# Moving the weight sums of a seven-product matrix scheme from VectorE to GpSimd, with more blocks under the scheme

## The chip, the cores and the metric

One core of one Trainium2 chip. Times are device microseconds for one launch of the whole program; the kernel before has a median of 2390.53 us over three runs.

## The reference

A two-layer encoder over one sequence of 256 tokens with 2048 features, all in float32. Each layer is a norm, a token mixer, a residual add, then a norm, a gated feed-forward part and a residual add. The change lies in the feed-forward part alone:

```python
def conv_glu(hn, w_up, conv_w, conv_b, w_down):
    u = hn @ w_up                       # 256 x 2048 times 2048 x 11008
    a, v = jnp.split(u, 2, axis=-1)
    ...                                 # c: depthwise convolution of width 3 over tokens
    return (jax.nn.gelu(c, approximate=False) * v) @ w_down     # 256 x 5504 times 5504 x 2048
```

## The kernel before

**Numbers in two halves.** TensorE multiplies in a reduced float32 form. Every operand is split into a high part, a cast by ACT (`wh`, `th`), and a low part, the difference made by VectorE (`wl`, `tl`). A product of two operands is then three matmuls: high by high, high by low, low by high (`product`, L237).

**Weights as a stream.** All weights pass through one stream of chunks. A raw piece of 128 x 2048 is loaded into one of three buffers `raw` by SP's queue, and split 1024 columns at a time into four buffers `wh` (L137, ACT) and `wl` (L138, VectorE). `stream` asks for pieces three ahead (`LOOK`). A scheduler orders the instructions of each engine when the program is built.

**Up and down chunks.** The feed-forward part of a layer works in two parts: 22 blocks of 128 hidden features, then 21. For each block there is an up chunk (32 pairs of matmuls at L328 and L332, then some ten small operations of VectorE and ACT, `done_up`, that give the block of activations `GT`). Behind the up chunks of a part come down chunks. Those of kind "st" compute a pair of 512-column outputs at once, from two blocks of hidden features (a unit) and both halves of the tokens: the first pair of columns in both parts (`w_d0`), the second pair in part 0 alone (`w_d1`). The rest of part 1 goes in ordinary chunks. So a layer has three such down chunks of 11 units; in part 1 the last unit is half as large.

**Units and couples.** A unit is a product of 2 x 2 blocks, A (activations) by B (weights). A regular unit takes eight products. A couple, one of the units listed in `SEVEN`, takes seven, by Strassen's scheme in Winograd's form: it needs four sums of weight blocks (T1 to T4, `weight_sums`) and four of activation blocks (S1 to S4, `token_sums`), each split in halves too. Four products' sums are kept in the PSUM tiles `psm_` over the whole chunk and added to the residual `hm` by `mid` behind the last couple (L546 to L554, the last two by GpSimd); the four `psa_` are added by `done` (L559).

**Where the weight sums are made.** For the six units in `STORED` of every down chunk, VectorE makes the sums during the up chunks. `prepare` is a side job with due times: `side` has a clock of its own, advanced as matmuls are issued by 10.4 per up chunk in ticks of 0.65, and a job that yields a number goes on that much later. It loads the couple's weights into `pth` (1 MB), makes three differences (L179, L182, L184: T1 to T4 in `ptl`), and stores 1 MB into a scratch tensor `tscr` in DRAM. In the down chunk `split_squares` loads them back (`T<-tscr`), and ACT and VectorE split them (`th`, L209; `tl`, L210). The block B12 itself is then not needed, so that a stored unit's raw piece has 1536 columns. Unit 9 of part 0's first chunk is not stored; its sums are made in the down chunk. The loads and stores share SP's queue with the raw loads, in order: an instruction that waits holds those behind it. The down chunk's first pieces are issued once `prepare` is through; what is left of it then is issued at once (`side.until`).

Of the kernel before, what the change touches and what calls it, by code (L numbers as in the profile page):

```python
# [48 lines left out]
SEVEN = (1, 2, 4, 5, 7, 8, 9), (1, 2, 4, 5, 7, 8), (1, 2, 4, 5, 7, 8)  # L49
STORED = (1, 2, 4, 5, 7, 8)  # L50
# [10 lines left out]
def trunk_kernel(ctx, tc, xT, x_d, fg_d, pp_d, cst_d, w_gate, w_first, w_aq, w_ak, w_av, w_ao, w_aout, w_ao2,  # L61
# [114 lines left out]
    def weight_sums(a, b, T, T_):  # L176

        B22, B21, B12 = a[:, 512:1024], b[:, 0:512], b[:, 512:1024]
        dve.tensor_tensor(T.rearrange("p (a b) -> p a b", a=2), B12.unsqueeze(1).broadcast_to([P, 2, 512]),  # L179
                          a.rearrange("p (a b) -> p a b", a=2), ALU.subtract)  # L180
        yield 2.5
        dve.tensor_tensor(T_[:, 0:512], B22, T[:, 0:512], ALU.subtract)  # L182
        yield 2.5
        dve.tensor_tensor(T_[:, 512:1024], B21, T_[:, 0:512], ALU.subtract)  # L184

    def split_squares(ch, parts):
# [4 lines left out]
        def raw(u):  # L191
            if u not in raws and u < units:
                raws[u] = load_raw(ch.src, 2048 * u, min(2048 * (u + 1), 1024 * ch.nk) - (512 if u in ch.stored else 0))
                if u in ch.stored:
                    kept[u] = [temporary(ch.pool, "T") for _ in range(2)]
                    for t, src in zip(kept[u], ch.stored[u]):
                        nc.sync.dma_start(t, src)
            return raws.get(u)

        def combine(u):  # L200
            r = raw(u)
            T, T_ = kept[u] if u in kept else (temporary(ch.pool, "T") for _ in range(2))
            if u not in kept:
                for _ in weight_sums(r[:, 0:1024], r[:, 1024:2048], T, T_):
                    pass
            sums[u] = []
            for i, t in enumerate((T, T_)):
                th, tl = (ch.pool.tile([P, 1024], F32R, tag=n, name=n) for n in (f"th{i}", f"tl{i}"))
                act.copy(th, t)  # L209
                dve.tensor_tensor(tl, t, th.bitcast(F32), ALU.subtract)  # L210
                sums[u].append((th, tl))

        for u in range(units):
            r = raw(u)
            if u + 1 in ch.seven and not ch.late:
                combine(u + 1)
            wh, wl = parts(r[:, 0:1024], 1024)
            yield wh, wl, 1
            if u + 1 in ch.seven and ch.late:
                combine(u + 1)  # L220
            if 2 * u + 1 < ch.nk:
                m = 512 if u in ch.seven else 1024
                wh, wl = parts(r[:, 1024:1024 + m], m)
                yield wh, wl, sums.pop(u, None)

    def squares_by_seven(ch, fetch, ready):
# [20 lines left out]
        for u in range(units):  # L247
# [3 lines left out]
            if 2 * u + 1 == ch.nk:  # L251
# [4 lines left out]
                break  # L256
            fetch()
            q = ready.pop(0)
            x0, x1 = ch.x(2 * u), ch.x(2 * u + 1)
            A11, A21, A12, A22 = half(x0, 0), half(x0, 1), half(x1, 0), half(x1, 1)  # L260
            B11, B22, B21 = block(p[:2], 0), block(p[:2], 1), block(q[:2], 0)
            if u in ch.seven:
                sx, t = ch.sums(u), q[2]
                S1, S3, S2, S4 = ((sx[:, i * P:(i + 1) * P], sx[:, 512 + i * P:512 + (i + 1) * P]) for i in range(4))
                T1, T3, T2, T4 = (block(t[i // 2], i % 2) for i in range(4))
                for i, (ps, x, w) in enumerate(((P1, A11, B11), (C12, S4, B22), (C11, A12, B21), (P5, S1, T1),
                                                (P7, S3, T3), (P6, S2, T2), (C21, A22, T4))):
                    product(ps, x, w, u == last and ps in psm_)
                    side.tick(0.65)
# [257 lines left out]
    def token_sums(mp, i, a, b, S):  # L527

        sx = mp.tile([P, 1024], F32R, tag=f"sx{i}", name="sx")
# [3 lines left out]
        act.copy(sx[:, 0:512], S)  # L533
        dve.tensor_tensor(sx[:, 512:1024], S, sx[:, 0:512].bitcast(F32), ALU.subtract)
        return sx
# [37 lines left out]
    def prepare(mp, todo, period, finished):  # L573

        yield 24.0
        for src, dst in todo:
            r, T = ([mp.tile([P, 1024], F32, tag=f"{n}{i}", name=f"p{n}") for i in range(2)] for n in ("th", "tl"))
            for i in range(2):
                late(r[i], src[:, i * 1024:(i + 1) * 1024])
            yield 9.0  # L580
            yield from weight_sums(*r, *T)
            for i in range(2):
                nc.sync.dma_start(dst[i], T[i])
            yield max(1.0, period - 14.0)
# [512 lines left out]
    def ffn(layer, norm, nxt):  # L1097
        stack = ExitStack()
        box = dict(n=3 * len(STORED) * layer)
# [10 lines left out]
        def done_up(f, i, GT, SX, seven):  # L1110
            def go(ps):
# [15 lines left out]
                if i % 2 and i // 2 in seven:  # L1127
                    SX[i // 2] = token_sums(mp, seven.index(i // 2), box["c"], c, avc[:, 0:2 * T])
# [3 lines left out]
        for part, (f0, nf) in enumerate(((0, FA), (FA, FB))):  # L1132
            GT, SX, todo, finished = [], {}, [], []

            def prep(todo=todo, finished=finished, nf=nf):
                if not pairs[0].pool:
                    begin()
                side.push(prepare(box["mp"], todo, (nf * 10.4 - 24.0) / len(todo) - 1.5, finished))

            for i in range(nf):  # L1140
                chunks.append(Chunk("fm", w_up[layer, f0 + i], KT, norm.x, done_up(f0 + i, i, GT, SX, SEVEN[2 * part]),
                                    prep if i == 0 else None,
                                    swap=(2,) if part and i == 0 else (3,) if f0 + i == 1 else (), paced=True))
            def two(src, c0, norm, seven, GT=GT, SX=SX, nf=nf, todo=todo, finished=finished):
                ch = pair(src, nf, c0, lambda k: GT[k], lambda u: SX[u], norm, seven)
                for u in STORED:
# [7 lines left out]
            chunks.append(two(w_d0[layer][:, f0 * 1024:(f0 + nf) * 1024], 0, nxt if part else None, SEVEN[2 * part]))  # L1154
# [4 lines left out]
            else:  # L1159
                chunks.append(two(w_d1[layer], 2, None, SEVEN[1]))  # L1160
# [103 lines left out]
def build(nc, ins, out_shape=(2, P, D), **kw):  # L1264
# [4 lines left out]
    tscr = nc.dram_tensor("tscr", (6 * len(STORED), 2, P, 1024), F32, kind="Internal").ap()  # L1269
# [18 lines left out]
```

## Time and profile before

| | |
|---|---|
| median of three runs | 2390.53 us (2390.34 to 2392.72) |
| span of the profiled execution, first to last instruction | 2388.5 us |
| TensorE busy | 2372.4 us, 99% |
| VectorE busy | 1944.1 us, 81% |
| ACT busy | 1298.8 us, 54% |
| GpSimd busy | 189.7 us, 8% |
| bytes read and written in DRAM | 512.69 MB, 39.91 MB |
| granted TensorE clock | 0.999 |

The runs give times of launches; the profiled execution is known by its span, and the median lies 2.0 us above that. In the profile's rows PE is TensorE, PEld its weight loads, DVE VectorE, POOL GpSimd, SP the queue that issues most DMAs, and L137 is line 137 of the kernel. A row of a group gives busy time, the mean time of one in ns, and behind the second bar the idle time of the engine before such instructions with what ended it.

### The profile page before, as it was taken

The page shows a single profiled execution, that of the slowest core. Times are in us where ns is not written, and L with a number is a line of the kernel's source. Part 1 is how long each engine was busy: PE and PEld are TensorE (multiplying, and loading weights), DVE is VectorE, ACT ScalarE, POOL GpSimd, SP SyncE. Part 2 cuts the span into 40 slices and gives each one's busy share as a digit, 9 for nine tenths or more (in the row PEclk, how much of TensorE's full clock was granted, in tenths as well). Part 3 has the DMA queues.
Part 4 walks back from the last instruction along what each step waited for, and adds up shares of the span by engine and source line. Part 5 has one row for each costly group of instructions (what it writes and reads, how often), then busy time and mean ns, then how long its engine had stood idle before and what let it go on. Part 6 is the DMA issues. An engine that isn't in the chain of part 4 may idle for free.

```text
span 2388.5 us, 37988 instructions
## 1 busy us (share of the span) xinstructions
PE 2372.4 (99%) x14614; PEld 2030.4 (85%) x14614; DVE 1944.1 (81%) x3221; ACT 1298.8 (54%) x2013; POOL 189.7 (8%) x240
## 2 busy tenths in 40 slices
PE   9999999999999999999999999999999999999998
PEld 7888888888888888888888888888888888888887
DVE  7766687988887888777888888888889888788874
ACT  7655455454564554555555555555555565454563
POOL 0100000000000000001222222220000000000000
PEclk9999999999999999999999999999999999999999
DMA  8654556988787777755554554545798888677774
GB/s 300 201 180 165 183 178 211 333 294 317 269 293 254 251 239 262 273 194 182 173 171 168 175 177 160 177 166 188 258 325 298 298 281 296 231 249 263 249 266 148
DMA packets 98789, 555.07 MB, mean 232 GB/s; under 512 B 11168, under 2 KB 11680, under 8 KB 50736
## 3 DMA queue, kind: packets, MB, share of 16 engines
q1 hardware_dynamic: 96912, 548.64, 65.6%
q0 software_dynamic: 1120, 3.21, 0.7%
q8 instruction: 114, 1.87, 0.3%
q10 hardware_dynamic: 576, 0.79, 0.1%
q14 instruction: 67, 0.55, 0.1%
HBM read 512.69 MB, written 39.91 MB: 231 GB/s over the span
## 4 chain that ended last, share of the span: by engine, by line
PE 98%; DVE 1%; issue 1%; DMA 0%; ACT 0%; SPq 0%; POOLq 0%; POOL 0%
PE mm L328 37%; PE mm L344 23%; PE mm L332 18%; PE pc L237 12%; PE mm L237 5%; PE pn L776 1%; PE py L1034 1%; PE pd L984 1%; PE pz L405 0%; PE pa L984 0%; DMA raw<-in_w_first 0%; PE S L762 0%; DVE tl L210 0%; PE pz L1055 0%; PE pa L1009 0%
## 5 line engine op out<-in xcount | busy, mean ns | idle before, releaser
L328 PE MATMUL mm<-xt,wh 128*128 128x512 f32 x3776 | 1313.4, 394 | 0.0
L137 ACT CAST wh<-raw 128x1024 fp32r<-128x1024 f32 (+1 forms) x846 | 853.5, 1019 | 693.8 <-PE mm L328 237.9
L138 DVE TENSOR_TENSOR wl<-raw,wh 128x1024 fp32r<-128x1024 f32 (+1 forms) x846 | 1004.7, 1195 | 265.1 <-ACT wh L137 257.6
L332 PE MATMUL mm<-xt,wl 128*128 128x256 f32 x3776 | 1045.9, 278 | 0.0
L328 PEld LDWEIGHTS mm<-xt,wh 128*128 128x128 f32 x3776 | 706.2, 188 | 159.4
L332 PEld LDWEIGHTS mm<-xt,wl 128*128 128x128 f32 x3776 | 709.5, 188 | 4.5 <-issue 0.4
L344 PE MATMUL mm<-wh,xt 128*128 128x512 f32 x1024 | 320.5, 391 | 3.0 <-ACT xt L350 1.3
L344 PEld LDWEIGHTS mm<-wh,xt 128*128 128x128 f32 x1024 | 191.4, 188 | 43.3 <-ACT xt L350 1.7
L344 PE MATMUL mm<-wl,xt 128*128 128x512 f32 x512 | 198.2, 391 | 0.0
L237 PE MATMUL pc<-wh,g 128*128 128x512 f32 x508 | 167.2, 389 | 0.0
L355 ACT COPY b<-mm 128x256 f32<-128x256 f32 x236 | 87.4, 370 | 122.9 <-PE mm L332 122.7
L210 DVE TENSOR_TENSOR tl<-T,th 128x1024 fp32r<-128x1024 f32 x88 | 109.9, 1264 | 38.9 <-ACT th L209 36.7
L209 ACT CAST th<-T 128x1024 fp32r<-128x1024 f32 x88 | 92.7, 1054 | 73.6 <-PE mm L237 43.5
L237 PEld LDWEIGHTS pc<-wh,g 128*128 128x128 f32 x508 | 95.4, 188 | 19.9
L344 PEld LDWEIGHTS mm<-wl,xt 128*128 128x128 f32 x512 | 96.2, 188 | 18.9
L553 POOL TENSOR_TENSOR hm<-hm,u 128x512 f32<-128x512 f32 x8 | 10.4, 1302 | 1150.9 <-DVE u L552 1150.9
L237 PE MATMUL pc<-wl,g 128*128 128x512 f32 x254 | 98.9, 389 | 0.0
L344 PE MATMUL mm<-wh,g 128*128 128x512 f32 x308 | 96.6, 392 | 0.0
L237 PE MATMUL mm<-th,sx 128*128 128x512 f32 x264 | 91.9, 390 | 0.0
L356 DVE TENSOR_TENSOR avc<-mm,b 128x256 f32<-128x256 f32 x172 | 72.0, 418 | 14.7 <-ACT b L355 14.7
L361 DVE TENSOR_TENSOR avc<-avc,R 128x256 f32<-128x256 f32 x172 | 71.9, 419 | 1.6
L976 DVE COPY kq<-QK 128x256 f32<-128x256 f32 x224 | 69.7, 336 | 0.0
(260 smaller groups left out, 2476.7 us busy)
## 6 DMA issues: line engine op xcount, KB each, us to landing
raw<-in_w_up SPq DMA_DIRECT2D x172, 1024.0 KB, 5.5
raw<-in_w_d SPq DMA_DIRECT2D x48, 1024.0 KB, 5.0
raw<-in_w_bq SPq DMA_DIRECT2D x48, 1024.0 KB, 4.9
pth<-in_w_d SPq DMA_DIRECT2D x72, 512.0 KB, 6.7
tscr<-ptl SPq DMA_DIRECT2D x72, 512.0 KB, 4.7
T<-tscr SPq DMA_DIRECT2D x72, 512.0 KB, 5.1
raw<-in_w_d SPq DMA_DIRECT2D x36, 768.0 KB, 5.2
raw<-in_w_ao SPq DMA_DIRECT2D x24, 1024.0 KB, 4.8
```

The lines of the kernel that those rows point to most:

```text
L137: pin(act.copy(wh[:, :m], r))
L138: pin(dve.tensor_tensor(wl[:, :m], r, wh[:, :m].bitcast(F32), ALU.subtract))
L209: act.copy(th, t)
L210: dve.tensor_tensor(tl, t, th.bitcast(F32), ALU.subtract)
L237: pe.matmul(ps, a, b, start=id(ps) not in begun, stop=stop and i == 2)
L328: pe.matmul(ps[f], wh[:, c:c + P], x, start=k + kk == 0, stop=False)
L332: pe.matmul(ps[f][:, 0:T], wl[:, c:c + P], x[:, 0:T], start=False, stop=k + kk == ch.nk - 1)
L344: pe.matmul(ps[t], x[:, a + t * P:a + (t + 1) * P], w[:, c], start=st and i == 0, stop=sp and i == 2)
L355: act.copy(b, ps[:, T:2 * T])
L356: dve.tensor_tensor(dst, ps[:, 0:T], b, ALU.add)
L361: dve.tensor_tensor(dst, dst, R, ALU.mult)
L976: dve.tensor_copy(m[:, j].rearrange("k (m p j) -> k m p j", p=2, j=h), blocks(z, h, 0, T))
```

## The change

- `SEVEN` is now units 1 to 9 for both down chunks of part 0, and 1, 2, 3, 5, 6, 7, 8 for part 1: 9, 9 and 7 couples a layer instead of 7, 6 and 6. All of them are stored; `STORED` is gone.
- `prepare` loads three of a couple's four blocks (1024 and 512 columns), makes three differences of 128 x 512 in place by GpSimd, and stores 1536 columns. T4 is not stored. The loads of the next couple are issued ahead of the stores of this one.
- In the down chunk a stored couple's pieces are four, not two with the sums in the second one: B11 and B22; T1 and T2 (`th0`, `tl0`); B21 and T3, split together as one piece of 1024, T3 being loaded into the raw piece; and T4. GpSimd makes T4 from B21 and T2 (128 x 512), ACT casts it, GpSimd makes its low half.
- The seven products of a stored couple come in the order of these pieces, the one with T4 last.
- S4, the fourth sum of activations, is put into the columns of `GT` that a couple doesn't read (part 0), or into a tile of its own (part 1), with a cast and a difference of 128 x 128 for itself.

```diff
-SEVEN = (1, 2, 4, 5, 7, 8, 9), (1, 2, 4, 5, 7, 8), (1, 2, 4, 5, 7, 8)
-STORED = (1, 2, 4, 5, 7, 8)
+SEVEN = tuple(range(1, 10)), (1, 2, 3, 5, 6, 7, 8)
...
     def split_squares(ch, parts):
...
-                raws[u] = load_raw(ch.src, 2048 * u, min(2048 * (u + 1), 1024 * ch.nk) - (512 if u in ch.stored else 0))
+                n = 1536 if u in ch.stored else min(2048, 1024 * ch.nk - 2048 * u)
+                raws[u] = load_raw(ch.src, 2048 * u, 2048 * u + n)
                 if u in ch.stored:
-                    kept[u] = [temporary(ch.pool, "T") for _ in range(2)]
-                    for t, src in zip(kept[u], ch.stored[u]):
-                        nc.sync.dma_start(t, src)
+                    kept[u] = temporary(ch.pool, "T")
+                    nc.sync.dma_start(kept[u], ch.stored[u][:, 0:1024])
+                    nc.sync.dma_start(raws[u][:, 1536:2048], ch.stored[u][:, 1024:1536])
...
         for u in range(units):
             r = raw(u)
-            if u + 1 in ch.seven and not ch.late:
-                combine(u + 1)
+            if u in ch.stored:
+                T4 = ch.pool.tile([P, 512], F32, tag="t4", name="t4")
+                pool.tensor_tensor(T4, r[:, 1024:1536], kept[u][:, 512:1024], ALU.subtract)
             wh, wl = parts(r[:, 0:1024], 1024)
             yield wh, wl, 1
+            if u in ch.stored:
+                th, tl = (ch.pool.tile([P, 1024], F32R, tag=n, name=n) for n in ("th0", "tl0"))
+                act.copy(th, kept[u])
+                dve.tensor_tensor(tl, kept[u], th.bitcast(F32), ALU.subtract)
+                yield th, tl, 0
...
             if 2 * u + 1 < ch.nk:
-                m = 512 if u in ch.seven else 1024
+                m = 512 if u in sums else 1024
                 wh, wl = parts(r[:, 1024:1024 + m], m)
                 yield wh, wl, sums.pop(u, None)
+            if u in ch.stored:
+                th, tl = (ch.pool.tile([P, 512], F32R, tag=n, name=n) for n in ("th1", "tl1"))
+                act.copy(th, T4)
+                pool.tensor_tensor(tl, T4, th.bitcast(F32), ALU.subtract)
+                yield th, tl, 0
...
     def squares_by_seven(ch, fetch, ready):
...
+            if u in ch.stored:
+                S1, S3, S2, S4 = ch.sums(u)
+                products((P1, A11, B11), (C12, S4, B22))
+                fetch()
+                t = ready.pop(0)
+                products((P5, S1, block(t[:2], 0)), (P6, S2, block(t[:2], 1)))
+                fetch()
+                q = ready.pop(0)
+                products((C11, A12, block(q[:2], 0)), (P7, S3, block(q[:2], 1)))
+                fetch()
+                t = ready.pop(0)
+                products((C21, A22, t[:2]))
...
     def prepare(mp, todo, period, finished):
...
-        yield 24.0
-        for src, dst in todo:
-            r, T = ([mp.tile([P, 1024], F32, tag=f"{n}{i}", name=f"p{n}") for i in range(2)] for n in ("th", "tl"))
-            for i in range(2):
-                late(r[i], src[:, i * 1024:(i + 1) * 1024])
-            yield 9.0
-            yield from weight_sums(*r, *T)
-            for i in range(2):
-                nc.sync.dma_start(dst[i], T[i])
-            yield max(1.0, period - 14.0)
+        loaded = []
+
+        def load(i):
+            if i < len(todo):
+                n = ("th", "tl")[i % 2]
+                r, b = (mp.tile([P, w], F32, tag=f"{n}{j}", name=f"p{n}") for j, w in enumerate((1024, 512)))
+                late(r, todo[i][0][:, 0:1024])
+                late(b, todo[i][0][:, 1536:2048])
+                loaded.append((r, b))
+
+        yield 20.0
+        load(0)
+        for i, (_, dst) in enumerate(todo):
+            yield period / 2
+            r, b = loaded[i]
+            for out, x, y in ((r[:, 0:512], b, r[:, 0:512]), (b, b, r[:, 512:1024]), (r[:, 512:1024], r[:, 512:1024], r[:, 0:512])):
+                pool.tensor_tensor(out, x, y, ALU.subtract)
+            yield period / 4
+            load(i + 1)
+            yield period / 4
+            nc.sync.dma_start(dst[:, 0:1024], r)
+            nc.sync.dma_start(dst[:, 1024:1536], b)
...
-                side.push(prepare(box["mp"], todo, (nf * 10.4 - 24.0) / len(todo) - 1.5, finished))
+                side.push(prepare(box["mp"], todo, (nf * 10.4 - 28.0) / len(todo), finished))
```

67 lines of the change are left out of this document (39 added, 28 removed).

## The prediction

> **What bounds the kernel now.** I read the page's busy shares and its chain first, then PE's waits.
>
> ```profile
> span 2388.5 us, 37988 instructions
> PE 2372.4 (99%) x14614; PEld 2030.4 (85%) x14614; DVE 1944.1 (81%) x3221; ACT 1298.8 (54%) x2013; POOL 189.7 (8%) x240
> PE 98%; DVE 1%; issue 1%; DMA 0%; ACT 0%; SPq 0%; POOLq 0%; POOL 0%
> PE mm L237 <- DVE tl L210: 0.6, 2, 0.3
> ```
>
> TensorE is busy for 2372.4 of 2388.5 us, and the chain lies on it for 98%. What feeds it hardly ever comes late: the wait for `tl`, a split operand of the down chunks, is 0.6 us in all. So a matmul that goes is worth its full pitch, but only as long as the feeding engines keep up. VectorE, at 81%, is the next one, and GpSimd with 8% looks free. The question is whether GpSimd's time is really free, so I looked next at how the two engines behave when they work at once, in the timeline around the end of a down chunk.
>
> ```profile
> 365.86 1.23 DVE L138 TENSOR_TENSOR wl<-raw,wh 128x1024 fp32r<-128x1024 f32 x1 [0.45 <-ACT wh L137]
> 367.76 1.31 POOL L553 TENSOR_TENSOR hm<-hm,u 128x512 f32<-128x512 f32 x1 [62.36 <-DVE u L552]
> 368.20 1.96 DVE L138 TENSOR_TENSOR wl<-raw,wh 128x1024 fp32r<-128x1024 f32 x1
> 369.03 2.29 POOL L554 TENSOR_TENSOR hm<-hm,u 128x512 f32<-128x512 f32 x1
> 370.08 0.68 DVE L559 TENSOR_TENSOR hm<-hm,pc 128x512 f32<-128x512 f32 x1
> 370.67 1.72 DVE L138 TENSOR_TENSOR wl<-raw,wh 128x1024 fp32r<-128x1024 f32 x1
> ...
> 694.16 1.30 POOL L553 TENSOR_TENSOR hm<-hm,u 128x512 f32<-128x512 f32 x1 [300.17 <-DVE u L552]
> 694.50 4.27 DVE L210 TENSOR_TENSOR tl<-T,th 128x1024 fp32r<-128x1024 f32 x2
> 695.41 2.29 POOL L554 TENSOR_TENSOR hm<-hm,u 128x512 f32<-128x512 f32 x1
> ...
> L553 POOL TENSOR_TENSOR hm<-hm,u x8: 1297/1302/1308, 367.8 to 2319.6; 128x512 f32<-128x512 f32 x8
> L554 POOL TENSOR_TENSOR hm<-hm,u x8: 2270/2286/2292, 369.0 to 2320.9; 128x512 f32<-128x512 f32 x8
> ```
>
> The columns are start, duration, engine, line, operation. Lines 553 and 554 are the same operation on the same shapes, one behind the other, and yet take 1.30 and 2.29 us, at all eight places. VectorE's split `wl` takes 1.23 us alone and 1.96 and 1.72 us here. The ends tell why. The first `wl` ends at 368.20 + 1.96 = 370.16; take 1.23 off and it began its work at 368.93, just where L553 ends. L554 ends at 371.32, which is 1.16 us after that `wl` ended. The next `wl` ends at 372.39, so it began at 371.16 to 371.18, as L554 ended. They take turns: neither runs while the other does. The operation L559 between them, which reads PSUM and only one SBUF tensor, took its usual 0.68 us in the middle of L554 and waited for nobody. In the second group, two `tl` and two GpSimd operations fill 694.16 to 698.77, that is 2.3 us for each pair.
>
> The Trainium skill, page "SBUF — State Buffer", section "Who interferes with whom", says the same as a rule: a VectorE instruction with two SBUF inputs contends with a GpSimd instruction that reads SBUF, the later one is blocked until the other is through, and one with at most one SBUF input isn't held. The rows agree (1.96 and 1.72 against 1.23; 0.68 unheld); by that rule GpSimd's new work is not beside VectorE's but in line with it.
>
> **The change part by part.**
>
> *Matmuls (gain).* A regular unit of a down chunk has 8 products of three matmuls, a couple 7. There are 25 couples a layer for 19, 50 for 38, so 12 products, 36 matmuls, go.
>
> ```profile
> 0.00:2388.00 2388.00, 413.68 (x1812) 339.40 (x1812) 1.00 0.67 232
> ```
>
> This row has the matmuls of L237 alone: 413.68 / 1812 = 0.2283 us each (a single one lasts 0.39, but they overlap). 36 x 0.2283 = 8.2 us. A couple is 21 x 0.2283 = 4.79 us of TensorE, a regular unit 24 x 0.2283 = 5.48.
>
> *Down chunks: what a couple now asks of the feeders.* Before, VectorE made `wl` of 1024 and of 512 columns and two `tl` of 1024. Now it makes two `wl` and one `tl` of 1024, and GpSimd makes T4 and the `tl` of T4, 128x512 each, both with two SBUF inputs.
>
> ```profile
> 709.13 2.36 DVE L210 TENSOR_TENSOR tl<-T,th 128x1024 fp32r<-128x1024 f32 x2 [0.66 <-ACT th L209]
> 617.00:728.00 111.00, 110.69 (x513) 91.98 (x512) 91.08 (x107) 67.21 (x80) 3.54 (x2) 1.00 0.83 292
> L138 DVE TENSOR_TENSOR wl<-raw,wh 128x512 fp32r<-128x512 f32 x12 | 8.2, 684 | 0.0
> L559 DVE TENSOR_TENSOR hm<-hm,pc 128x512 f32<-128x512 f32 x4 | 2.6, 676 | 0.0
> L209 ACT CAST th<-T 128x1024 fp32r<-128x1024 f32 x24 | 25.3, 1054 | 23.8 <-PE mm L237 13.5 <-PE pc L237 6.1 <-DMA T<-tscr 3.9
> ```
>
> Two operations of 1024 in 2.36 us, where one takes 1.22, make a pitch of 1.14; so the couple costs VectorE 3 x 1.14 = 3.42 us instead of 3.42 + 0.60. GpSimd's two cost by the rows above from 2 x 1.02 (370.16 to 371.18) to 2 x 1.16 (a pair's 2.30 less 1.14). In line that is 5.46 to 5.74 us a couple against 4.79 of TensorE: the feeders become slower than the matmuls, where before they needed 4.02. ACT's three casts of 1.05 and one of about half that, 3.7 us, stay below.
>
> For the two down chunks of part 0 of a layer, back to back (the row 617 to 728 is about that stretch before: VectorE 91.1 us, GpSimd 3.5 of 111), the line is: VectorE 18 couples x 3 + 4 regular units x 2 = 62 splits x 1.14 = 70.7; the adds to `hm` at the first chunk's end, nine from PSUM at 0.62 (L559: 2.6 for four) and one more, 6.2; the last up chunk's ten small operations, about 0.39 each, 3.9; GpSimd 36 + 2 operations, 38.8 at 1.02 or 44.1 at 1.16. Sum 119.6 to 124.9. The PSUM-fed ones (5.6 there and two of the small ones, 0.8) need not stand in line: 113.2 to 118.5 if they all run beside GpSimd. VectorE starts with a lead of three pieces (3.4) and must be done one piece (2.7) before TensorE: 0.7 off. TensorE needs 18 x 4.79 + 4 x 5.48 = 108.1. The stall is 4.4 to 16.1 us; I take 9.7, with 1.16 (the longest run of turns in the trace) and the PSUM-fed ones beside.
>
> The chunk of part 1 has seven couples with a regular unit after three: 28 splits x 1.14, 14 x 1.16 and 3.9 are 52.1 against 7 x 4.79 + 3 x 5.48 + 2.7 = 52.7. It fits; only its four couples in a row outrun the lead, 4 x 0.95 = 3.8 against 3.4. I take 0.5 (0 to 1). The regular units absorb the rest.
>
> *Up chunks.* Three VectorE operations a couple go, three GpSimd operations of 128x512 come, in place and each waiting for the one before.
>
> ```profile
> 400.00:600.00 200.00, 200.00 (x1156) 174.81 (x1155) 175.47 (x291) 101.19 (x149) 0.00 (x0) 1.00 0.86 311
> L138 DVE TENSOR_TENSOR wl<-raw,wh 128x1024 fp32r<-128x1024 f32 x72 | 87.8, 1220 | 7.7 <-ACT wh L137 7.1
> L356 DVE TENSOR_TENSOR avc<-mm,b 128x256 f32<-128x256 f32 x36 | 15.0, 417 | 2.2 <-ACT b L355 2.2
> L179 DVE TENSOR_TENSOR ptl<-pth 128x1024 f32<-128x1024 f32 x12 | 14.7, 1225 | 14.2 <-DMA pth<-in_w_d 12.9 <-issue 1.3
> L182 DVE TENSOR_TENSOR ptl<-pth,ptl 128x512 f32<-128x512 f32 x12 | 8.2, 683 | 0.0
> L184 DVE TENSOR_TENSOR ptl<-pth,ptl 128x512 f32<-128x512 f32 x11 | 7.5, 683 | 0.0
> L532 DVE TENSOR_TENSOR avc<-avc 128x128 f32<-128x128 f32 x20 | 5.7, 287 | 0.3
> L534 DVE TENSOR_TENSOR sx<-avc,sx 128x512 fp32r<-128x512 f32 x5 | 3.4, 684 | 0.0
> ```
>
> In 200 us, 18 chunks (72 splits, four each, so 11.1 us a chunk), VectorE is busy 175.5. Of that 14.7 + 8.2 + 7.5 less overlaps, about 27.6, goes; token sums for two more couples and the short splits add about 5 (1.83 a couple by L532 and L534, 0.29 for each short one): 153. GpSimd's period is 12.35 in the side jobs' clock of 10.4 a chunk ((228.8 - 28) / 18 = 11.16, its parts rounded up to ticks of 0.65), so 13.2 us, 15.2 couples in 200 us, 45.5 operations x 1.16 = 53. In line that is 206 of 200; with L356, PSUM-fed, beside it, 191. So 0 to 7 us for the 244 us of part 0, nearer the lower end, since GpSimd's part has no due time of its own: I take 2. Part 1, seven couples in place of six in 231 us, has room.
>
> *Queues.* On SP the stores now wait for GpSimd, and a weight load is queued behind each. Bytes hardly grow: 1.5 MB for each of 25 couples a layer in the up chunks, where 18 took 2 MB each. A couple's load lands in about 6.7 us and its sums take 3.5 to 6.9, and the raw loads have three buffers of 5.5 us each, so I cost this at nothing; if that cover is gone, see the third rival.
>
> ```profile
> pth<-in_w_d SPq DMA_DIRECT2D x72, 512.0 KB, 6.7
> ```
>
> *Sum.* Per layer 9.7 + 0.5 + 2 = 12.2; twice 24.4; less 8.2: +16.2. Against the profiled span that is 2388.5 + 16.2 = 2404.7, and with the 2.0 us by which the median of the runs (2390.53) lies above that span, 2407. With all lower ends it is 2 x 4.4 - 8.2 = +0.6, 2391; with the upper ends 2 x (16.1 + 1 + 7) - 8.2 = +40, 2430.5.
>
> **The rivals.**
>
> *Faster: the queue of ready pieces hides it.* The 36 matmuls go and nothing stalls: 2390.5 - 8.2 = 2382.3. For it: `tl` was held to 2.3 us at 694.50 while VectorE had no gap, and TensorE waited 0.6 us in all; four `wh`/`wl` buffers can hold more lead than three pieces. Against it: that lead is spent once, while 18 couples overrun by 0.67 to 0.95 each. It decides if the lead is some 10 us, or if the two engines overlap more than the rows show. Chance 0.28.
>
> *Much slower: GpSimd gets its turn only when VectorE has nothing to do.* Then a couple goes step by step.
>
> ```profile
> 1133.50 2.86 POOL L949 TENSOR_TENSOR QK<-q,G 128x256 f32<-128x256 f32 x1 [8.38 <-DVE G L948]
> 1134.01 1.21 DVE L138 TENSOR_TENSOR wl<-raw,wh 128x1024 fp32r<-128x1024 f32 x1
> L949 POOL TENSOR_TENSOR QK<-q,G x32: 727/780/2859, 1114.6 to 1571.7; 128x256 f32<-128x256 f32 x32
> ```
>
> Here GpSimd's operation of 0.78 us stood for 2.86 while VectorE's later ones ran at their usual time. If T4 is held like that, ACT stands at T4's cast and VectorE runs dry: 3.42 + 1.16 + 0.62 + 1.16 = 6.36 us a couple, 1.57 over, 50 times, less six leads of 3.4, is 58; with 4 for the up chunks and the 8.2 off, 2390.5 + 54 = 2444. Against it: T4 is issued at the head of its unit. Chance 0.11.
>
> *The sums are not all made in the up chunks.* 18 periods of 12.35 and the first 20 are 242 of the 228.8 that part 0 has, so the last couple's load, sums and stores are issued at the down chunk's head. SP then holds the second unit's loads for 6.7 + 3 x 2.3 = 13.6 us. Three raw buffers (16.6) cover that, unless they are partly used up: up to 5 us a layer on top, 2417. Chance 0.09.
>
> **How the numbers follow.** The forecast has 0.52, of which 0.12 lies within 0.2% of the median (4.8 us, about what a measurement of this kernel can tell from no change), at its lower end, and 0.40 above. Faster is the first rival, 0.28; slower 0.40 + 0.11 + 0.09 = 0.60. Cases of both signs are likely: the forecast's own range is 2391 to 2431. The range over the cases reaches from the first rival, 2381, to the forecast's upper end, 2431, and leaves out the second rival and some of the tails.
>
> **What would show it.** 36 fewer matmuls in the trace; L553's kind of GpSimd operation at 1.2 to 2.3 us in both stages; mean `wl` and `tl` in the down chunks well above 1.22 us; TensorE waits for `tl` or `wl` of some 10 us in the two down chunks of part 0, little in part 1. The forecast is wrong if couples follow each other at 4.79 us through all nine, or if `wl` stays at 1.22 beside GpSimd's subtractions.

## The result, and the profile after

The changed kernel takes 2455.56 us (median of four runs, 2454.59 to 2459.31) against 2390.57 before: slower, by a factor of 1.0273 (95% interval 1.0259 to 1.0287). The direction was forecast; the size was not: 65 us more instead of 16, above the range's upper end of 2431.

The page of the kernel after, its busy shares and its chain:

```profile
span 2453.2 us, 38360 instructions
PE 2396.5 (98%) x14578; PEld 2028.6 (83%) x14578; DVE 2054.0 (84%) x3143; ACT 1321.1 (54%) x2075; POOL 634.3 (26%) x490
PE 75%; DMA 7%; DVE 6%; POOL 5%; issue 5%; ACT 1%; SPq 1%; POOLq 0%; ACTq 0%; DVEq 0%
```

The 36 matmuls are gone (14614 to 14578), and yet the chain lies on TensorE for 75% where it was 98%. Transfers, VectorE and GpSimd now have stretches of it. VectorE has 78 operations fewer and is busy for 110 us more: its operations have become longer.

Where the time went is seen best by stretches with the same work in them. First the up chunks of part 0 in layer 0, after and before (columns: stretch, its length, busy time and instructions of PE, PEld, DVE, ACT, POOL, then granted clock, DMA share, GB/s):

```profile
370.00:650.00 280.00, 271.12 (x1515) 232.93 (x1515) 254.25 (x362) 139.82 (x224) 93.69 (x56) 0.99 0.76 277
```

```profile
370.00:635.00 265.00, 265.00 (x1516) 230.77 (x1515) 230.71 (x384) 141.39 (x216) 2.01 (x2) 1.00 0.80 287
```

The same number of matmuls takes 280 us instead of 265. Next the two down chunks of part 0 behind them, the matmuls of `product` alone (PE, PEld), before and after, both layers:

```profile
635.40:747.20 111.80, 111.45 (x489) 91.48 (x489) 1.00 0.79 279
1925.00:2036.70 111.70, 111.44 (x489) 91.41 (x489) 1.00 0.79 280
```

```profile
650.70:782.80 132.10, 116.86 (x474) 87.76 (x474) 0.99 0.74 255
1971.70:2103.30 131.60, 115.87 (x474) 86.72 (x474) 1.00 0.75 264
```

15 matmuls fewer, 20 us longer. Some of the next up chunk's matmuls are done in the gaps, so that the fair measure reaches from the first matmul of these chunks to the first one of part 1's down chunk:

```profile
635.45 0.39 PE L237 MATMUL pc<-wh,g 128*128 128x512 f32 x1
980.01 0.40 PE L237 MATMUL pc<-wh,g 128*128 128x512 f32 x1
```

```profile
650.74 0.40 PE L244 MATMUL pc<-wh,g 128*128 128x512 f32 x1
1011.99 0.39 PE L244 MATMUL pc<-wh,g 128*128 128x512 f32 x1
```

344.6 us became 361.2 (layer 1, in the same way: 344.5 became 360.7). I call this the down stretch, and the one ahead of it, from the first matmul of the mixer's output chunk, the up stretch: 311.7 became 326.7, and 313.5 became 331.1. With the gain of 15 x 0.2283 = 3.4 us that a down stretch should have had, the losses are 15.0 and 17.6 us in the up stretches, 20.0 and 19.6 in the down stretches. The rest of the program is 0.8 us shorter in sum, but not everywhere. Part 1's down chunk with the ordinary chunks behind it (up to the first `pa` matmul, a product of layer 1's mixer, or in layer 1 up to the end) takes 1.4 and 1.7 us more with one product of 0.7 us fewer, so it loses 2.1 and 2.4. The mixer of layer 1, which has the same matmuls in both kernels, is 4.2 us shorter, and no run says why.

Some of TensorE's longer stalls cost more than their own length. One such place in the kernel after, and the stretch behind it:

```profile
643.83 0.58 PE L357 MATMUL mm<-xt,wl 128*128 128x256 f32 x1 [2.32 <-DVE wl L137]
```

```profile
643.60:647.00 3.40, 3.17 (x10) 2.79 (x11) 3.37 (x6) 1.04 (x1) 1.32 (x1) 0.50 1.03 416
```

For 3.4 us the granted clock (third figure from the end) is 0.50, and matmuls of 512 columns start 0.43 us apart instead of 0.23. The same follows stalls that end at 697.8 and 1920.1 us; from the last matmul's start to the next one's these three are 2.26 to 2.71 us long. Two others of 2.26 and 2.32 us (ending at 596.7 and 1969.1) have no such stretch behind them. By these figures each of the three costs some 1.6 us more, an estimate of 5 of the 65 us.

**Why the up chunks lose.** The waits of the kernel after in its up stretch (engine, line, what it waited for: us in all, times, longest):

```profile
ACT wh L136 <- DMA raw<-in_w_up: 48.3, 24, 4.8
```

SP's own queue there:

```profile
SPq L625 <- POOL ptl L620: 68.5, 9, 9.5
SPq L625 <- POOL pth L620: 67.2, 9, 10.0
```

and ACT's wait in the kernel before:

```profile
ACT wh L137 <- DMA raw<-in_w_up: 4.5, 3, 2.3
```

SP stands 135.7 us, 7.5 us for each of the 18 couples, at a store (L625) that waits for GpSimd, and ACT waits 44 us longer in all for raw weights than it did. One such case in SP's timeline, and the same moment in the chain (start, length, what):

```profile
542.88 0.74 SPq L391 DMA_DIRECT2D raw<-in_w_up  x1
553.29 0.33 SPq L625 DMA_DIRECT2D tscr<-pth  x1
553.72 0.38 SPq L391 DMA_DIRECT2D raw<-in_w_up  x1
```

```profile
542.36 7.71 DMA pth<-in_w_d
550.21 1.64 POOL pth L620
551.91 1.36 POOL pth L620
553.29 0.33 SPq L625
553.72 5.45 DMA raw<-in_w_up
559.26 1.06 ACT wh L136
560.34 1.23 DVE wl L137
```

The couple's own load lands after 7.7 us, two of GpSimd's differences follow, the store is issued, and only then, 10.8 us after the raw load before it, the next raw load, which ACT is waiting for.

**What the down chunks show.** VectorE's splits there, two rows of the kernel before (635 to 747 us) and two of the kernel after (650 to 783 us; busy, mean ns, idle before them):

```profile
L138 DVE TENSOR_TENSOR wl<-raw,wh 128x1024 fp32r<-128x1024 f32 x31 | 38.2, 1250 | 5.7 <-ACT wh L137 5.2
L210 DVE TENSOR_TENSOR tl<-T,th 128x1024 fp32r<-128x1024 f32 x24 | 30.6, 1300 | 12.0 <-ACT th L209 11.4
```

```profile
L137 DVE TENSOR_TENSOR wl<-raw,wh 128x1024 fp32r<-128x1024 f32 x46 | 67.7, 1506 | 19.3 <-ACT wh L136 19.3
L219 DVE TENSOR_TENSOR tl<-T,th 128x1024 fp32r<-128x1024 f32 x18 | 26.0, 1444 | 0.9 <-ACT th L218 0.9
```

and the waits of GpSimd and ACT in the same stretch (650 to 783 us):

```profile
POOL tl L230 <- ACT th L229: 53.6, 18, 6.4
ACT wh L136 <- DMA raw<-in_w_d: 26.2, 11, 4.6
```

`wl` has a mean of 1.51 us, 1.25 before: the turns are there as forecast. But VectorE also idles for 19.3 us and ACT waits 26.2 us for raw weights, which a stretch bound by the two engines' sum alone would not show. One couple in the timeline:

```profile
692.01 0.61 ACT L229 CAST th<-t 128x512 fp32r<-128x512 f32 x1
692.61 1.21 DVE L219 TENSOR_TENSOR tl<-T,th 128x1024 fp32r<-128x1024 f32 x1
692.69 2.27 POOL L230 TENSOR_TENSOR tl<-t,th 128x512 fp32r<-128x512 f32 x1 [2.23 <-ACT th L229]
695.05 1.28 POOL L213 TENSOR_TENSOR t<-raw,T 128x512 f32<-128x512 f32 x1
696.36 0.33 SPq L128 DMA_DIRECT2D raw<-in_w_d  x1
696.75 1.04 ACT L136 CAST wh<-raw 128x1024 fp32r<-128x1024 f32 x1 [4.13 <-DMA raw<-in_w_d]
```

GpSimd gets T4's cast, is held by VectorE's `tl` for 1.1 us, makes the low half, then the next T4, and the end of T4 lets SP issue a raw load.

### The profile page after: what moved, and what is told of

It is laid out like the page before. It is cut to its first block, busy times and chain, and to the rows that moved or that the text cites. A ratio compares the mean times of both kernels' runs of the same rounds, so it can differ in the third digit from the quotient of the medians.

```text
span 2453.2 us, 38360 instructions
## 1 busy us (share of the span) xinstructions
PE 2396.5 (98%) x14578; PEld 2028.6 (83%) x14578; DVE 2054.0 (84%) x3143; ACT 1321.1 (54%) x2075; POOL 634.3 (26%) x490
## 4 chain that ended last, share of the span: by engine, by line
PE 75%; DMA 7%; DVE 6%; POOL 5%; issue 5%; ACT 1%; SPq 1%; POOLq 0%; ACTq 0%; DVEq 0%
PE mm L353 27%; PE mm L369 22%; PE mm L357 14%; PE pc L244 5%; DVE wl L137 3%; DMA raw<-in_w_up 2%; PE mm L244 2%; POOL t L213 2%; POOL tl L230 2%; DMA ptl<-in_w_d 2%; DMA raw<-in_w_d 1%; DMA pth<-in_w_d 1%; POOL ptl L620 1%; PE pn L817 1%; ACT wh L136 1%
## 5 line engine op out<-in xcount | busy, mean ns | idle before, releaser
L137 DVE TENSOR_TENSOR wl<-raw,wh 128x1024 fp32r<-128x1024 f32 (+1 forms) x846 | 1114.0, 1325 | 276.8 <-ACT wh L136 271.9
L136 ACT CAST wh<-raw 128x1024 fp32r<-128x1024 f32 (+1 forms) x846 | 870.8, 1037 | 675.8 <-PE mm L369 153.6
L620 POOL TENSOR_TENSOR pth<-pth 128x512 f32<-128x512 f32 x78 | 138.7, 1778 | 345.1 <-DMA pth<-in_w_d 328.7
L620 POOL TENSOR_TENSOR ptl<-ptl 128x512 f32<-128x512 f32 x72 | 121.3, 1685 | 276.1 <-DMA ptl<-in_w_d 272.0
L244 PE MATMUL pc<-wh,g 128*128 128x512 f32 x412 | 146.8, 396 | 6.1 <-ACT wh L136 6.1
L230 POOL TENSOR_TENSOR tl<-t,th 128x512 fp32r<-128x512 f32 x50 | 94.0, 1881 | 153.3 <-ACT th L229 153.3
L213 POOL TENSOR_TENSOR t<-raw,T 128x512 f32<-128x512 f32 x50 | 89.2, 1784 | 71.7 <-DMA T<-tscr 66.1
L244 PEld LDWEIGHTS pc<-wh,g 128*128 128x128 f32 x412 | 77.4, 188 | 27.0 <-ACT wh L136 11.9
L529 POOL TENSOR_TENSOR rs<-rs,mhalf 128x2 f32<-128x2 f32 x24 | 16.6, 696 | 318.4 <-DVE rs L528 318.4
L1162 ACT ACTIVATE avc<-avc 128x256 f32<-128x256 f32 x86 | 36.0, 418 | 111.2 <-DVE avc L1161 111.0
L386 DVE TENSOR_TENSOR avc<-avc,R 128x256 f32<-128x256 f32 x172 | 89.4, 520 | 3.0
```

Of the source, the lines that this page charges most:

```text
L136: pin(act.copy(wh[:, :m], r))
L137: pin(dve.tensor_tensor(wl[:, :m], r, wh[:, :m].bitcast(F32), ALU.subtract))
L213: pool.tensor_tensor(T4, r[:, 1024:1536], kept[u][:, 512:1024], ALU.subtract)
L230: pool.tensor_tensor(tl, T4, th.bitcast(F32), ALU.subtract)
L244: pe.matmul(ps, a, b, start=id(ps) not in begun, stop=stop and i == 2)
L386: dve.tensor_tensor(dst, dst, R, ALU.mult)
```

## The experiments

Two questions stood: are the up chunks slow by the turns of the two engines (line) or by SP's queue (queue), and what of the down chunks' loss hangs on GpSimd. The losses below are those of the up and down stretches of layer 0 and layer 1 as defined above, each against the matmuls it has.

**Stores in GpSimd's queue** (`store_pool`).

```diff
-            nc.sync.dma_start(dst[:, 0:1024], r)
-            nc.sync.dma_start(dst[:, 1024:1536], b)
+            pool.dma_start(dst[:, 0:1024], r)
+            pool.dma_start(dst[:, 1024:1536], b)
```

> The changed kernel, with the stores of the weight sums issued from GpSimd's own queue, not from SP's: no raw load stands behind a store that waits for GpSimd. GpSimd's arithmetic stays. Theory 1 (line: VectorE and GpSimd take turns, and their sum is too long) expects no gain, 2450 to 2460 us. Theory 2 (queue: SP, held by stores that wait for GpSimd, brings the raw loads late in the up chunks) expects the some 33 us that the two up stretches of part 0 lost to come back: about 2423 us.

2428.45 us (1.0158, 1.0142 to 1.0173). The up stretches lose 2.1 and 3.3 us instead of 15.0 and 17.6, the down stretches are as they were. ACT's wait in the up stretch is gone, with GpSimd's arithmetic untouched:

```profile
ACT wh L136 <- DMA raw<-in_w_up: 2.0, 2, 1.5
```

So the up chunks' loss was the queue; 2 to 3 us are left there for the turns.

**VectorE in GpSimd's place**, in the up chunks (`up_dve`), in the down chunks (`down_dve`), in both (`all_dve`).

```diff
 in prepare (up_dve, all_dve)
-                pool.tensor_tensor(out, x, y, ALU.subtract)
+                dve.tensor_tensor(out, x, y, ALU.subtract)
 in split_squares (down_dve, all_dve)
-                pool.tensor_tensor(T4, r[:, 1024:1536], kept[u][:, 512:1024], ALU.subtract)
+                dve.tensor_tensor(T4, r[:, 1024:1536], kept[u][:, 512:1024], ALU.subtract)
...
-                pool.tensor_tensor(tl, T4, th.bitcast(F32), ALU.subtract)
+                dve.tensor_tensor(tl, T4, th.bitcast(F32), ALU.subtract)
```

> The changed kernel, with the three differences of a couple in the up chunks made by VectorE. GpSimd still works in the down chunks. Theory 1: VectorE's 153 us of 200 and 45 operations at 0.6 are 180 of 200, nothing lost in the up chunks: 2455.6 - 33 = 2423 us. Theory 2: the stores still stand in SP's queue and now wait for VectorE, as before the change, for a shorter time: 2423 to 2440 us.

> The changed kernel, with T4 and its low half made by VectorE in the down chunks; GpSimd still makes the sums in the up chunks. A couple costs VectorE 3 x 1.14 + 2 x 0.60 = 4.62 us, below TensorE's 4.79. Both theories expect the down chunks' loss to go (20 us for the two chunks of part 0 and 2.6 for that of part 1, in each layer): about 2410 us. If VectorE in line is too slow even so (the adds of the chunk's end on top), 2415 to 2425.

> The changed kernel with no GpSimd arithmetic in up or down chunks at all: VectorE makes the three differences in place and T4 with its low half. 9, 9 and 7 couples as in the changed kernel. If all the loss hangs on GpSimd, by the line or by the queue, only the 36 matmuls' gain is left: 2382 to 2386 us. If the couples' number or their order of pieces costs something itself, more than 2390.

`up_dve` 2425.57 (1.0146, 1.012 to 1.0173): the up stretches lose 0.0 and 0.4 us. The stores of VectorE's sums don't hold SP long enough to matter: SP stands 79.0 us at all stores of layer 0's up stretch, against 155.8 in the changed kernel (L624 and L625) and 73.6 in the kernel before. `down_dve` 2443.30 (1.0219, 1.0203 to 1.0234): only 12 us better than the changed kernel, where 2410 to 2425 had been expected. Its down stretches still lose 16.4 and 21.9 us (stretches at half clock follow there once in layer 0 and three times in layer 1), so that VectorE in the down chunks alone gains next to nothing there. `all_dve` 2404.82 (1.006, 1.0045 to 1.0075): 51 us of the 65 hang on GpSimd, 32 of them in the up stretches, 13 in the down stretches, some 4 in part 1's down chunks. But the down stretches still lose 10.4 + 3.4 = 13.8 us and 13.2, which the prediction had at nothing: nine couples in a row cost something without GpSimd's arithmetic too.

**Who holds the raw loads in the down chunks?** T4 reads the raw buffer. In `dve_noraw` and `pool_noraw` it is made from T1 and T2 alone; in `dve_early` and `pool_early` T4 has two buffers and is issued a unit ahead (a smaller tile for S4 makes room).

```diff
 dve_noraw (on all_dve), pool_noraw (on store_pool)
-  tensor_tensor(T4, r[:, 1024:1536], kept[u][:, 512:1024], ALU.subtract)
+  tensor_tensor(T4, kept[u][:, 0:512], kept[u][:, 512:1024], ALU.subtract)
 dve_early (on all_dve), pool_early (on store_pool)
-                T4 = ch.pool.tile([P, 512], F32, tag="t4", name="t4")
+                t = ch.pool.tile([P, 512], F32, tag="t4", bufs=2, name="t4")
...
+            if u + 1 in ch.stored:
+                T4s[u + 1] = fourth(u + 1)
```

> The kernel without GpSimd arithmetic (VectorE makes all sums; 2404.8 us), with T4 made from the loaded T1 and T2 alone, not from B21, so that the raw buffer is free as soon as its two splits are done. It leaves out: the true T4. Number, size and engine of all operations stay. Theory A (the raw buffer, held until T4, brings the next raw load late: it was issued 6.6 us after the one before and landed 6.8 us later, just when ACT wanted it) expects the couples to follow at TensorE's 4.79 us: 2382 to 2387. Theory B (VectorE's 4.62 us a couple in line, with the adds on top, is too slow) expects no change, 2402 to 2407. Theory C (DRAM can't bring 1.5 MB per 4.79 us) also expects no change.

> The kernel without GpSimd arithmetic, with two buffers for T4 and T4 of the next unit issued at the head of a unit, so that it need not wait for the low half of the T4 before it and gives up its raw buffer sooner. Nothing is left out. Theory A expects most of the 18 us between 2404.8 and 2382.3 back: 2383 to 2392. Theories B and C expect 2402 to 2407.

> The changed kernel with the stores in GpSimd's queue (2428.5 us), and T4 made by GpSimd from T1 and T2 alone, so that GpSimd holds no raw buffer. It leaves out: the true T4. VectorE and GpSimd still take turns as often as before. What is left above 2382 is the price of the turns themselves. The line of the prediction has 10.2 us a layer in the down chunks: 2403. If the raw buffers were all of it: 2383 to 2390. If the turns are all of the down chunks' loss: 2425 to 2430.

> The changed kernel with the stores in GpSimd's queue, two buffers for T4, and T4 of the next unit issued at the head of a unit. Nothing is left out; GpSimd makes all sums as in the changed kernel. As for the run before: 2403 by the line of the prediction, some us more where T4 still comes late; 2383 to 2392 if the held raw buffers were all of it.

2405.98, 2406.46, 2431.31 and 2426.66 us: none moves by more than its interval's width from the kernel it is made from (2404.8 and 2428.5; the first less 2382.3 is 22.5, not the 18 of one expectation). So the held raw buffer is not all of the loss, for either engine.

The total hides a part, though. In some of these kernels TensorE is slower in part 1's up chunks, which lie in the down stretch behind the couples and have the same matmuls in every kernel. `all_dve` and `dve_noraw` there:

```profile
800.00:900.00 100.00, 100.00 (x579) 88.15 (x578) 84.64 (x150) 51.63 (x80) 0.00 (x0) 1.00 0.72 243
```

```profile
800.00:900.00 100.00, 100.00 (x568) 86.69 (x567) 83.53 (x149) 51.05 (x79) 0.00 (x0) 1.00 0.70 239
```

Both are busy without a gap at a clock of 1.00, and yet `dve_noraw` gets 11 of 579 matmuls fewer done: 1.9%, an estimate of some 4 us over the 21 up chunks of 11.1 us. `light`, `light_free`, `light_clean`, `dve_free`, `pool_memset`, `eight_break` and `pool_pairs` below have this slower pitch (567 to 569) in both layers, `pool_noraw` in layer 1, all other kernels in neither. What sets it isn't shown. Without these 4 us `dve_noraw` loses some 9 and 11 us in its down stretches where `all_dve` loses 13.8 and 13.2, and `pool_noraw` some 19 and 19 where `store_pool` loses 20.4 and 21.8. `dve_early` loses 11.1 and 15.5, `pool_early` 18.8 and 17.4. By these single executions the held raw buffer makes up a few us a layer.

**A GpSimd that doesn't read** (`pool_memset`, on `store_pool`).

```diff
-                pool.tensor_tensor(T4, r[:, 1024:1536], kept[u][:, 512:1024], ALU.subtract)
+                pool.memset(T4, 0.5)
...
-                pool.tensor_tensor(tl, T4, th.bitcast(F32), ALU.subtract)
+                pool.memset(tl.bitcast(F32), 0.0)
```

> The changed kernel with the stores in GpSimd's queue (2428.5 us), with both GpSimd operations of a couple in the down chunks made fills of 128x512, which read nothing. It leaves out: T4. GpSimd still works and still stands in the chain, but doesn't read SBUF. If the turns of two readers are the price in the down chunks, VectorE's splits fall from a mean of 1.5 back to 1.22 us and the time to that of the kernel whose VectorE has 3.42 us a couple, 2385 to 2400. If any GpSimd work beside VectorE costs, 2420 to 2430.

2403.36 us (1.0051, 1.0035 to 1.0067), 25 us less than with the subtractions, a little above the first expectation. Its down stretches lose 8.5 and 8.5 us, of which some 4 are the slower pitch; its up stretches lose 5.6 and 5.0, each with one stretch of 3.4 us at half clock. In its down chunks:

```profile
L137 DVE TENSOR_TENSOR wl<-raw,wh 128x1024 fp32r<-128x1024 f32 x43 | 51.7, 1222 | 12.4 <-ACT wh L136 11.8
L219 DVE TENSOR_TENSOR tl<-T,th 128x1024 fp32r<-128x1024 f32 x17 | 21.0, 1233 | 15.4 <-ACT th L218 15.1
```

VectorE's splits are back at 1.22 us, beside a GpSimd that writes as many columns as before. The Trainium skill, page "SBUF — State Buffer", section "Who interferes with whom", has it so: a two-input VectorE instruction contends with a GpSimd instruction that reads SBUF, not with one that only writes it. The fills are shorter too, the one in the low half's place doesn't wait for ACT's cast, and the one in T4's place holds no raw buffer (a few us a layer by `pool_noraw`), so that the 25 us are the price of the turns with all that hangs on them, not of the lock's time alone.

**What is left without GpSimd.** `light`, `light_free` and `light_clean` take VectorE's two operations on T4 away; `no_t_load` loads T1 and T2 once a chunk, and `dve_free` does so with the raw buffer free as well. All stand on `all_dve`.

```diff
 light, light_free (T4 = r[:, 1536:2048] or kept[u][:, 0:512], read by ACT in T4's place)
-                dve.tensor_tensor(tl, T4, th.bitcast(F32), ALU.subtract)
-                yield th, tl, 0
+                act.copy(tl[:, 0:1], T4[:, 0:1])
+                yield th, th, 0
 light_clean
-                act.copy(th, T4)
-                dve.tensor_tensor(tl, T4, th.bitcast(F32), ALU.subtract)
-                yield th, tl, 0
+                act.copy(th, kept[u][:, 0:512])
+                yield th, th, 0
 no_t_load; dve_free has dve_noraw's T4 besides
-                    kept[u] = temporary(ch.pool, "T")
-                    nc.sync.dma_start(kept[u], ch.stored[u][:, 0:1024])
+                    kept[u] = kept[min(kept)] if kept else temporary(ch.pool, "T")
+                    if len(kept) == 1:
+                        nc.sync.dma_start(kept[u], ch.stored[u][:, 0:1024])
```

> The kernel without GpSimd arithmetic (2404.8 us), with VectorE's two 128x512 operations a couple taken away: T4 is read from T3's place and its high half stands for its low half. It leaves out: T4 and its low half. A couple then costs VectorE 3.42 us against TensorE's 4.79. If VectorE in line is what is left of the loss: 2382 to 2387. If DRAM traffic (the same bytes) or the number of couples in a row sets it: 2400 to 2406.

> The kernel without GpSimd arithmetic (2404.8 us), with T1 and T2 loaded once in a down chunk and used for all its couples: 0.5 of a couple's 1.5 MB are not loaded. It leaves out: the other couples' T1 and T2. VectorE's work stays. If the transfers set what is left of the loss: 2382 to 2390. If VectorE does: 2400 to 2406.

> The kernel without GpSimd arithmetic (2404.8 us), with both bonds of the loads cut: T4 is made from T1 and T2 alone, so that it holds no raw buffer, and T1 and T2 are loaded once a chunk, so that no load of theirs stands in SP's queue ahead of a raw load. It leaves out: the true T4 and the other couples' T1 and T2. VectorE's work stays, 4.62 us a couple. If late raw loads are all that is left of the loss: 2382 to 2387. If VectorE in line is: 2398 to 2406.

> The kernel without GpSimd arithmetic, with VectorE's two 128x512 operations a couple taken away and no raw buffer held in their place: T4's cast reads T1, and its high half stands for its low half. It leaves out: T4 and its low half. All loads stay. VectorE has 3.42 us a couple. If VectorE in line is what is left of the loss: 2382 to 2388. If the loads of T1 and T2, ahead of the raw loads in SP's queue, or DRAM's rate are: 2396 to 2406.

> The kernel without GpSimd arithmetic and with nine couples in a row (2404.8 us), with T4's two 128x512 operations of VectorE taken away and no other instruction put in their place: the cast of T1's columns stands for both halves of T4, and no raw buffer is held for it. It leaves out: T4. All loads stay. VectorE has 3.42 us a couple. If VectorE in line is what is left of the loss: 2382 to 2388. If the loads or the order of ACT's and SP's queues are: 2396 to 2406.

2414.85, 2400.66, 2402.66, 2414.05 and 2402.74 us. The first and the fourth say nothing about VectorE: the small cast that stands in for T4's low half waits in ACT's own queue for a transfer, ahead of casts that TensorE needs, 8.6 us in three waits between 684 and 708 us of `light_free`:

```profile
ACT tl L229 <- DMA T<-tscr: 8.6, 3, 5.4
```

In `light` ACT's small cast waits in the same way, 6.0 us in four waits between 637 and 760 us, for the load of T3 (`raw<-tscr`). `light_clean`, with nothing in its place, answers: with VectorE at 3.42 us a couple the kernel is 2 us faster than with 4.62. A third of a couple's bytes less buys 4 us (`no_t_load`), the free raw buffer on top nothing in the total. Without the slower pitch the down stretches lose some 8.5 and 8 us in `light_clean`, 10.6 and 11.7 in `no_t_load`, and some 7.5 and 8 in `dve_free`, against 13.8 and 13.2 in `all_dve`. `light_clean` holds no raw buffer either, and `dve_noraw` has 9 and 11 by that alone. So by these single executions the loads and the held buffer each have a part in these 14 us, VectorE's work a smaller one, and none of them, taken alone, makes them up.

**Fewer couples in a row** (on `all_dve`).

```diff
-SEVEN = tuple(range(1, 10)), (1, 2, 3, 5, 6, 7, 8)
+SEVEN = (1, 2, 4, 5, 7, 8, 9), (1, 2, 4, 5, 7, 8)            # seven_old
+SEVEN = (1, 2, 3, 4, 6, 7, 8, 9), (1, 2, 3, 5, 6, 7, 8)      # eight_break
+SEVEN = (1, 2, 3, 5, 6, 8, 9), (1, 2, 3, 5, 6, 7, 8)         # pairs_break
```

> The kernel without GpSimd arithmetic, with the couples of part 0 at units 1, 2, 4, 5, 7, 8, 9 in both chunks and of part 1 at 1, 2, 4, 5, 7, 8: 20 a layer, nearly the 19 of before. By matmuls alone 2390.5 - 2 x 0.69 = 2389. If it is the unbroken row of couples that costs, 2387 to 2391; if it is the pieces' order or the stores and loads in place, 2394 to 2400.

> The kernel without GpSimd arithmetic, with one regular unit in the middle of part 0's chunks: couples at 1 to 4 and 6 to 9, part 1 as in the changed kernel, 23 a layer. Nothing is left out. By matmuls alone 2390.5 - 8 x 0.69 = 2385. If the length of an unbroken row is what costs (four outrun the lead by little), 2385 to 2390; if each couple beyond some rate costs, 2393 to 2400.

> The kernel without GpSimd arithmetic, with couples at 1, 2, 3, 5, 6, 8, 9 in part 0's chunks and as in the changed kernel in part 1, 21 a layer. Nothing is left out. By matmuls alone 2390.5 - 4 x 0.69 = 2387.8; 2386 to 2390 if two regular units in the row give VectorE and the loads the room to catch up.

2390.41 (1.0001, 0.9991 to 1.001), 2406.30 (1.0065, 1.0048 to 1.0082) and 2387.27 us (0.9983, 0.9974 to 0.9992). With 20 or 21 couples a layer next to nothing is lost (1.7 and 0.6 us in a down stretch); `pairs_break` gains 3.6 us on the 2390.83 that stood beside it, where the matmuls' count gives 2.7, and is 0.17% faster than the kernel before. With one more couple in each of part 0's chunks, in two rows of four, a down stretch loses 11.4 and 10.5 us, of which some 4 are the slower pitch: above both expectations. In `pairs_break`'s two chunks TensorE has hardly any gaps (the same columns as before, matmuls of `product`):

```profile
636.10:747.60 111.50, 110.92 (x486) 90.56 (x484) 1.00 0.77 278
```

**GpSimd with room** (`pool_pairs`: `store_pool` with the couples of `pairs_break`).

```diff
-SEVEN = tuple(range(1, 10)), (1, 2, 3, 5, 6, 7, 8)
+SEVEN = (1, 2, 3, 5, 6, 8, 9), (1, 2, 3, 5, 6, 7, 8)
```

> The changed kernel with GpSimd making all sums, the stores in its own queue, and couples at 1, 2, 3, 5, 6, 8, 9 in part 0's chunks, 21 a layer. Nothing is left out. In line, VectorE and GpSimd need 58 x 1.14 + 10.1 + 30 x 1.16 = 111 us for two chunks, 104.6 with what PSUM feeds beside it, against 14 x 4.79 + 8 x 5.48 = 110.9 of TensorE. If the line's sum is what counts, the down chunks lose next to nothing: 2387.8 and the some 5 us that GpSimd's turns cost the up chunks, 2390 to 2396. If every couple with GpSimd in its chain costs, as in the changed kernel, 14/18 of that: 2410 to 2420.

2401.92 us (1.0046, 1.0031 to 1.0061), 26.5 less than with nine couples in a row and 14.7 more than `pairs_break`. The turns are as long as ever:

```profile
L137 DVE TENSOR_TENSOR wl<-raw,wh 128x1024 fp32r<-128x1024 f32 x47 | 68.8, 1500 | 10.7 <-ACT wh L136 10.6
```

Its up stretches lose nothing (0.0 and -0.1), its down stretches 5.5 + 0.7 = 6.2 and 5.5. The time fits neither of the two expectations, but the mechanism is the first one's: part 1's up chunks have the slower pitch here (568 matmuls in the 100 us, `pairs_break` 579), so that some 4 us of each down stretch are no stall, and only 1 to 2 us are left for the down chunks. Another 2.1 and 1.6 us more than in `pairs_break` lie in part 1's down chunks and what follows them, where the couples stand as in the changed kernel.

## Why the prediction was wrong

*The matmuls' gain* of 8.2 us: the trace has 36 matmuls fewer, and `pairs_break`, where next to nothing stalls, got 3.6 us for twelve (2.7 by the count), 1.9 of them in layer 1's mixer, which loses no product.

*The line of VectorE and GpSimd*, 9.7 us a layer in part 0's down chunks: the mechanism holds (`wl` 1.25 to 1.51 us, and back to 1.22 beside a GpSimd that doesn't read). Its reading of the ends is a little rough: L553 ends at 369.07 and not 368.93, L554 at 371.32 and not 371.16 to 371.18, so the turns fit to some 0.15 us. With room in the row (`pool_pairs`) the sum is right too. With nine couples in a row the size fails: 20.0 and 19.6 were lost. The sum counted engine time alone. Nine couples in a row lose 13.8 and 13.2 us with no GpSimd arithmetic at all, though VectorE's 4.62 us a couple lie under TensorE's 4.79; GpSimd adds some 6 to that in the changed kernel. I had costed the longer row itself at nothing. And the two prices don't add up: with room in the row GpSimd costs 1 to 2 us, without its reading the long row costs 8.5, of which 4 are the slower pitch, and with GpSimd out of the down chunks alone (`down_dve`) 16.4 and 21.9 stay.

*The up chunks*, 2 us a layer by the line: `store_pool` shows 2.1 and 3.3, so this term was about right.

*The queues*, costed at nothing: this step failed worst, for 13 and 14 of the up stretches' 15.0 and 17.6 us. I had set a store's wait of up to 13.6 us against three raw buffers of 5.5 each. But of these 16.6 us one buffer is being split and a raw load takes 5.6 to land, so that some 5.5 are left, less than the 7.5 that SP stood at a mean L625. This is a working, not a measurement, and a mean alone doesn't decide it: the kernel before stood 6.1 us a couple at its stores and had ACT wait 4.5 us in all, but with twelve couples in that stretch and not eighteen. The third rival had the same mechanism, but only for the last couple of a part, at 5 us; that case didn't come (the last stores leave 4 to 6 us ahead of the chunk's first matmul), and the mechanism holds for every couple.

*Part 1 at 0.5 us* (0 to 1): too low as well. 2.1 and 2.4 us were lost there with GpSimd, 0.0 and 0.3 in `all_dve`.

*The rivals.* The faster one falls: the lead of pieces hid nothing like 18 couples' excess. The second, 2444, came nearest in time, but by another way: it laid 58 us on GpSimd's hand-over in the down chunks and 4 on the up chunks, where the runs have 40 (part 0) and 33.

What stays open: why a row of four to nine couples loses some 7 to 14 us a layer without GpSimd's arithmetic. Its raw loads come late, and to free the raw buffer, to load a third of the bytes less or to spare VectorE the added work brings back a part each; no run takes all three away at once. Each of these edits also gives another built order of all instructions, which no run here separates. Open too is what makes the matmuls of part 1's up chunks 1.9% slower in some of these orders.

## What to carry to other kernels

An idle engine's busy share says nothing on whether its work is free: look in the trace for a place where both engines work at once, and read the lengthened instructions and their ends. When work moves to a slower engine, follow every instruction that waits for it into the queue it stands in, and set its wait against what the buffers cover after the next transfer's own time is taken off. A sum of engine times gives a lower bound of a stall; a row of dense units needs regular ones between, and here two of them in eleven bought more than the products they cost. And before two kernels are compared by their time, compare a stretch that has the same instructions in both: here such a stretch differed by 4 us a layer, and hid what an edit elsewhere had gained.

## What was not expected of the hardware

Taking turns lengthens GpSimd's operations more than VectorE's (1.25 to 1.51 us in the mean): T4's subtraction of 128x512 has a median of 2.15 us beside VectorE, 1.28 at the least, in the kernel after:

```profile
L213 POOL TENSOR_TENSOR t<-raw,T x50: 1280/2147/2164, 651.3 to 2372.5; 128x512 f32<-128x512 f32 x50
```

while a fill of the same size, which reads nothing, takes 0.53 us and leaves VectorE's splits at 1.22.

```profile
660.27 0.53 POOL L213 MEMSET t<- 128x512 f32 x1 [1.30 <-ACT th L229]
```

Two things of TensorE were not expected either. A stall of over 2 us was followed, in three places of the kernel after, by 3.4 us at half the clock. And the same matmuls, without a gap and at a clock of 1.00, ran 1.9% slower in some kernels than in others (568 against 579 in 100 us).
